# The two SwiGLU output projections of a trunk layer, computed as seven Strassen products instead of plain blocks

## The chip, the core and the metric

One core of one Trainium2 chip runs the whole program. The metric is the device time of one execution in microseconds (us). Five engines work at once and wait for each other through semaphores: TensorE (PE) multiplies matrices into PSUM, VectorE (DVE) and ScalarE (ACT) work elementwise, GpSimd (POOL) does elementwise work in SBUF only, and SyncE (SP) issues all DMA transfers of this kernel from one queue. Each engine takes its instructions in the order in which they were written for it.

## The reference, cut to what matters

A trunk layer has two SwiGLU blocks with a mixing block between them. There are 1280 tokens: 1024 latent ones and 256 of context. The change concerns `@ w_out` inside `swiglu`, where the inner dimension is D_FF = 2816 and the output has D_MODEL = 1024 features.

```python
def swiglu(x, w_in, w_out):
    a, b = jnp.split(x @ w_in, 2, axis=-1)
    return (jax.nn.silu(a) * b) @ w_out

def trunk_layer(x, cvec, lp, ctx):
    ...
    h = rmsnorm(x, lp['norm_g'][0]) * (1.0 + sc1) + sh1
    x = x + 0.5 * g1 * swiglu(h, lp['ffn_w_in'][0], lp['ffn_w_out'][0])
    h = rmsnorm(x, lp['norm_g'][1]) * (1.0 + sc2) + sh2
    ...
    x = x + g2 * y
    h = rmsnorm(x, lp['norm_g'][2]) * (1.0 + sc3) + sh3
    x = x + 0.5 * g3 * swiglu(h, lp['ffn_w_in'][1], lp['ffn_w_out'][1])
```

## The kernel before

**Layout.** Activations lie with features on the 128 partitions and tokens along the free dimension. The tokens come in three chunks: `CHUNKS` 0 and 1 are 512 latent tokens each, chunk 2 is the 256 context tokens. `x[c][d]` is the residual stream of chunk c, feature tile d of 8; it is in SBUF during a projection. A matrix product keeps float32 accuracy with three float32r matmuls: an operand is split into a rounded part (a cast on ACT: `whi`, `uh`) and the rest (a subtraction on DVE: `wlo`, `ul`), and high by high, high by low and low by high are added up in PSUM.

**Stages.** `up(0)` computes silu(a)·b of the first SwiGLU, 22 inner tiles j one after the other, by seven products each (`seven`, on 512 latent tokens and half of the 1024 input features) and two plain context products; it writes the results to `ud` in DRAM. `down(0)` is the second projection. Then come the norm (`norm_chunk`), the input projection of the mixing block (its first products are called `pa_`), the mixing stages, the output projection, `up(1)` and `down(1)`, whose result is stored as `out_yT`. The program below calls `down(0)` the first half and `down(1)` the second half.

**The projection, `down`.** It runs over 11 blocks of two inner tiles (`BL = 2`). In a block it loads two rows of `w2` of 1024 columns and the two matching rows of `ud`, splits them, and for each chunk and each of 8 feature tiles accumulates six matmuls in one PSUM tile `po`. DVE then multiplies this tile by the gate and adds it to `x` (a SCALAR_TENSOR_TENSOR `x<-po,modT,x`). So in each block every tile of `x` is updated once: 264 updates in a projection. After the last block of a chunk, `done` is called: in the first half the norm of this chunk, in the second half the stores.

**Tiles.** `HG` hands out 40 buffers of 128x512 (raw loads `ur` among them), `TG` 28, of which 20 hold `x` during a projection. `whi` and `wlo` have 4 buffers each of 1024 columns. PSUM has two pools of 4 banks, `PG` and `PT_`.

**Order of work.** The program is first written down as a list; then a list scheduler (`Plan.issue`) sets the order of each engine with costs and latencies of its own (`price`, `LAT`): it takes the earliest written instruction that is ready when an engine becomes free. So an edit in one place can move instructions in others. All instructions are issued from one line, 394, which is why rows of the profile are told apart by the names of their tiles.

**Modulation.** While `up(0)` runs, `mod_half` computes 7 of the 9 modulation vectors beside it, in 112 portions: POOL multiplies twice (`pr<-wh,cb`, `wh<-wh,cb`), ACT sums up each product, and DVE adds the two sums to `modT` (128x2).

## Time and profile before

| what | value |
|---|---|
| time, median of 3 runs | 2585.28 us (2583.64 to 2587.88) |
| profiled execution | 2589.14 us, span 2587.4 us |
| PE busy | 2491.5 us, 96% of the span |
| DVE busy | 1762.7 us, 68% |
| ACT busy | 1011.8 us, 39% |
| POOL busy | 572.3 us, 22% |
| read from and written to HBM | 195.11 MB and 61.87 MB, 99 GB/s over the span |

The span runs from the first to the last instruction; the time of an execution has 1.7 us more around it. A busy PE is not a PE at its peak, since matmuls overlap: the pitch from start to start says what one costs. The profiled execution is 3.9 us above the median of the three runs.

### The profile page before, as it was taken

The numbers are of one execution on the slowest core, as the hardware profiler recorded it, in microseconds if no ns is written. First come the engines' busy times: TensorE is split into PE (matmuls) and PEld (weight loads), VectorE is DVE, ScalarE is ACT, GpSimd is POOL, SyncE is SP. The second block draws the span as 40 slices with busy tenths as digits, with TensorE's granted clock in tenths as the row PEclk, the third lists the DMA queues.
The fourth block names the chain that finished last, engine by engine and source line by source line (L and its number), as shares of the span: only waits on it lengthen the run. The fifth ranks groups of instructions, "written<-read, shape, count | busy, mean of one in ns | idle before, by whom it ended". The sixth has DMA issues, their size and how long they took to land.

```text
span 2587.4 us, 37285 instructions
## 1 busy us (share of the span) xinstructions
PE 2491.5 (96%) x14100; PEld 2096.2 (81%) x14100; DVE 1762.7 (68%) x2819; ACT 1011.8 (39%) x2009; POOL 572.3 (22%) x475
## 2 busy tenths in 40 slices
PE   5899999999999999999999989979999999999999
PEld 3688888888888878888778778868888888888888
DVE  7988888876877674568656575385555555587765
ACT  6555555543212046242476685252222222232110
POOL 1578778830000031122100263130000000000000
PEclk8899999999999999999999999979999999999999
DMA  7143444435422132341301234212122221362312
GB/s 262 60 141 118 146 126 143 124 104 185 150 78 86 49 106 68 103 124 66 109 31 36 81 114 142 98 37 80 54 80 67 66 74 60 97 234 86 94 50 82
DMA packets 146676, 259.42 MB, mean 100 GB/s; under 512 B 15936, under 2 KB 61504, under 8 KB 146496
## 3 DMA queue, kind: packets, MB, share of 16 engines
q1 hardware_dynamic: 146496, 257.04, 31.0%
q8 instruction: 111, 1.82, 0.3%
q14 instruction: 69, 0.57, 0.1%
HBM read 195.11 MB, written 61.87 MB: 99 GB/s over the span
## 4 chain that ended last, share of the span: by engine, by line
PE 74%; DVE 4%; ACT 2%; DMA 1%; issue 1%; POOL 0%; SPq 0%; ACTq 0%
PE po L394 23%; PE p_t L394 12%; PE p_b L394 9%; PE px L394 6%; PE pwo L394 4%; PE fb L394 3%; PE pgd L394 3%; PE ptb L394 2%; PE pyb L394 2%; PE ps L394 2%; PE pd L394 1%; DVE x L394 1%; ACT prob L394 1%; DVE dst L394 1%; PE pgate L394 1%
## 5 line engine op out<-in xcount | busy, mean ns | idle before, releaser
L394 DVE SCALAR_TENSOR_TENSOR x<-po,modT,x 128x512 f32<-128x512 f32 (+1 forms) x528 | 345.3, 661 | 159.7 <-PE po L394 158.4
L394 PE MATMUL po<-uh,whi 128*128 128x512 f32 (+1 forms) x1056 | 377.5, 358 | 5.1 <-DVE x L394 5.1
L394 ACT CAST whi<-raw 128x1024 fp32r<-128x1024 f32 x206 | 213.7, 1048 | 424.7 <-PE px L394 142.2
L394 PE MATMUL po<-uh,wlo 128*128 128x512 f32 (+1 forms) x1056 | 375.3, 355 | 0.0
L394 PE MATMUL po<-ul,whi 128*128 128x512 f32 (+1 forms) x1056 | 373.2, 353 | 0.0
L394 DVE TENSOR_TENSOR wlo<-raw,whi 128x1024 fp32r<-128x1024 f32 x206 | 281.3, 1366 | 100.4 <-ACT whi L394 96.1
L394 PEld LDWEIGHTS po<-uh,whi 128*128 128x128 f32 x1056 | 199.7, 189 | 32.2 <-DVE x L394 5.8
L394 PEld LDWEIGHTS po<-uh,wlo 128*128 128x128 f32 x1056 | 199.3, 189 | 30.9
L394 PEld LDWEIGHTS po<-ul,whi 128*128 128x128 f32 x1056 | 199.5, 189 | 29.5
L394 PE MATMUL px<-hh,whi 128*128 128x256 f32 x704 | 200.2, 285 | 2.3 <-ACT uc L394 1.2
L394 PE MATMUL px<-hl,whi 128*128 128x256 f32 x704 | 200.0, 284 | 0.7 <-DVE hl L394 0.7
L394 PE MATMUL px<-hh,wlo 128*128 128x256 f32 x704 | 198.8, 282 | 0.0
L394 POOL TENSOR_TENSOR pr<-wh,cb 128x512 f32<-128x512 f32 x112 | 172.8, 1543 | 92.3 <-DMA wh<-in_wmodT 60.7
L394 POOL TENSOR_TENSOR wh<-wh,cb 128x512 f32<-128x512 f32 x112 | 186.6, 1666 | 8.8
L394 ACT CAST uh<-ur 128x512 fp32r<-128x512 f32 x110 | 67.3, 622 | 301.7 <-DMA ur<-ud 248.0
L394 POOL TENSOR_TENSOR sq<-sq,sq 128x512 f32<-128x512 f32 (+1 forms) x32 | 37.9, 1185 | 495.3 <-ACT sq L394 492.3
L394 PEld LDWEIGHTS px<-hh,whi 128*128 128x128 f32 x704 | 135.1, 192 | 6.8 <-ACT hh L394 1.6
L394 PEld LDWEIGHTS px<-hl,whi 128*128 128x128 f32 x704 | 134.8, 192 | 5.4 <-DVE hl L394 1.3
L394 PEld LDWEIGHTS px<-hh,wlo 128*128 128x128 f32 x704 | 134.5, 191 | 0.5
L394 ACT ACTIVATE g<-g 128x512 f32<-128x512 f32 x88 | 55.6, 632 | 177.7 <-DVE g L394 177.6
L394 ACT ACTIVATE pr<-pr 128x512 f32<-128x512 f32 x112 | 70.9, 633 | 83.4 <-POOL pr L394 71.4
L394 ACT ACTIVATE wh<-wh 128x512 f32<-128x512 f32 x112 | 70.5, 629 | 56.6 <-POOL wh L394 55.8
(511 smaller groups left out, 6113.3 us busy)
## 6 DMA issues: line engine op xcount, KB each, us to landing
raw<-in_w SPq DMA_DIRECT2D x132, 512.0 KB
wh<-in_wmodT SPq DMA_DIRECT2D x112, 256.0 KB
ur<-ud SPq DMA_DIRECT2D x88, 256.0 KB
ud<-v SPq DMA_DIRECT2D x44, 256.0 KB
ud<-u SPq DMA_DIRECT2D x44, 256.0 KB
x<-in_xT SPq DMA_DIRECT2D x32, 256.0 KB
wmt<-in_wmod SPq DMA_DIRECT2D x32, 256.0 KB
xs<-x SPq DMA_DIRECT2D x32, 256.0 KB
```

The source lines that it names most:

```text
L394: getattr(real, meth)(*[f(v) for v in a], **{q: f(v) for q, v in k.items()})
```

## The change

Both projections are computed as one 2x2 block product: the inner dimension is cut into two halves of 11 tiles (`HF`), the output features into two halves of four tiles, and the latent tokens are chunks 0 and 1. Seven passes make the seven Strassen products, each over 11 inner tiles, with four PSUM tiles that collect the whole inner sum; one more pass (the fourth) has no latent product. The operands of five passes are sums or differences of weight tiles or activation tiles (`s1` to `s4`, `t1` to `t4`); DVE makes them as 128x512 tiles, and some are kept (`keep`) for a later pass. A finished PSUM tile is added to the outputs that need this product, 1 to 4 of them. The context is not part of it: half of its features are computed beside the first two passes with the same split weights (`pc`), the other half in the fourth pass. Splits of weights are now 512 columns wide. `done` is called for a chunk and a half of its features; in the first half all three norms are written behind the last pass, and the `pa_` products take the context chunk first. The addition to `modT` goes from DVE to POOL. Two small tables are written down in another place.

```diff
@@ -595,7 +595,7 @@
         S.activation(pr, pr, AF.Identity, accum_out=part[:, 0:1])
         G.tensor_tensor(w, w, cbs[0][:, 1], ALU.mult)
         S.activation(w, w, AF.Identity, accum_out=part[:, 1:2])
-        V.tensor_tensor(modT[:, s, f], part, modT[:, s, f] if hf else smv("bmod", 8 * s + f).to_broadcast([P, 2]),
+        G.tensor_tensor(modT[:, s, f], part, modT[:, s, f] if hf else smv("bmod", 8 * s + f).to_broadcast([P, 2]),
                         ALU.add)
         if hf and f == KT - 1:
             mod_finish(s)
@@ -705,7 +705,8 @@
-    BL = 2
+    HF = NFF // 2
     RAW = 2
     rawp = None
     ud = dp.tile([NFF, P, T], F32, name="ud")
@@ -821,40 +822,133 @@
             if after_unit:
                 after_unit()
-    def down(n, gate, src, after_block=None, done=None):
-        nb = NFF // BL
-        for b in range(nb):
-            js = [b * BL + jj for jj in range(BL)]
-            us = [[None] * 3 for _ in js]
...
-            for c, (t0, w) in enumerate(CHUNKS):
-                v = 1 if c == 2 else 0
-                for d in range(KT):
-                    po = PG("po")
-                    ds_ = slice(d * P, (d + 1) * P)
-                    for i in range(BL):
-                        (uh, ul), (hi, lo) = us[i][c], wo[i]
-                        TE.matmul(po[:, :w], hi[:, ds_], uh, start=(i == 0), stop=False)
-                        TE.matmul(po[:, :w], hi[:, ds_], ul, start=False, stop=False)
-                        TE.matmul(po[:, :w], lo[:, ds_], uh, start=False, stop=(i == BL - 1))
-                    V.scalar_tensor_tensor(x[c][d], po[:, :w], modT[:, gate, d, v:v + 1], x[c][d], ALU.mult, ALU.add)
-                if b == nb - 1:
-                    done(c)
+    def down(n, gate, src, done):
+        w2 = I["w2"][n]
+        c11, c12, c21, c22 = (0, 0), (1, 0), (0, 1), (1, 1)
+        lo, hi = slice(0, 512), slice(512, 1024)
+        keep = {}
+        def get(src_):
+            r = HG(name="ur")
+            dma(r, src_)
+            return r
+        def b(k, half, cols):
+            return get(ud[HF * half + k][:, cols])
+        def a(k, half, cols):
+            return get(w2[HF * half + k][:, cols])
+        def less(p, q, out):
+            V.tensor_tensor(out, p, q, ALU.subtract)
+            return out
+        def s1(k):
+            p, q = a(k, 0, hi), a(k, 1, hi)
+            V.tensor_tensor(p, p, q, ALU.add)
+            keep["s", k] = p
+            return p
+        def t1(k):
+            p = b(k, 0, hi)
+            keep["t", k] = less(p, b(k, 0, lo), p)
+            return p
+        def s2(k):
+            return less(keep["s", k], a(k, 0, lo), keep["s", k])
+        def t2(k):
+            return less(b(k, 1, hi), keep["t", k], keep["t", k])
+        def t4(k):
+            p = b(k, 1, lo)
+            return less(p, keep["t", k], p)
+        def s3(k):
+            p = a(k, 0, hi)
+            return less(p, a(k, 0, lo), p)
+        def t3(k):
+            p, q = b(k, 0, hi), b(k, 1, hi)
+            keep["b", k] = q
+            return less(p, q, p)
+        def s4(k):
+            p = a(k, 1, lo)
+            return less(p, keep["s", k], p)
+        PASSES = [
+            (lambda k: a(k, 1, lo), lambda k: b(k, 1, lo), [c11], (1, 0)),
+            (lambda k: a(k, 0, lo), lambda k: b(k, 0, lo), [c11, c12, c21, c22], (0, 0)),
+            (s1, t1, [c12, c22], None),
+            (lambda k: a(k % HF, k // HF, hi), None, [], (0, 1)),
+            (s2, t2, [c12, c21, c22], None),
+            (lambda k: a(k, 1, hi), t4, [c21], None),
+            (s3, t3, [c21, c22], None),
+            (s4, lambda k: keep["b", k], [c12], None),
+        ]
+        left = {}
+        for _, _, outs, _ in PASSES:
+            for o in outs:
+                left[o] = left.get(o, 0) + 1
+        def products(ps, wh, wl, q0, uh, ul, first, last):
+            for d in range(4):
+                q = slice(q0 + d * P, q0 + (d + 1) * P)
+                TE.matmul(ps[d], wh[:, q], uh, start=first, stop=False)
+                TE.matmul(ps[d], wh[:, q], ul, start=False, stop=False)
+                TE.matmul(ps[d], wl[:, q], uh, start=False, stop=last)
+        def update(c, f, p):
+            v = 1 if c == 2 else 0
+            V.scalar_tensor_tensor(x[c][f], p, modT[:, gate, f, v:v + 1], x[c][f], ALU.mult, ALU.add)
+        pc = None
+        for i, (ws, us, outs, context) in enumerate(PASSES):
+            nk = NFF if us is None else HF
+            ps = [(PG if i in (0, 1, 3, 5, 7) else PT_)(name="po") for _ in range(4)] if us is not None else None
+            if i in (0, 3):
+                pc = [(PT_ if i == 0 else PG)(name="pc")[:, :256] for _ in range(4)]
+            for k in range(nk):
+                q0 = 512 * (k % 2)
+                if context:
+                    if k % 2 == 0:
+                        j = k + HF * context[0] if us is not None else k
+                        m = min(2, nk - k)
+                        r, ch, cl = HG(name="ur"), HG(F32R, "uch"), HG(F32R, "ucl")
+                        dma(r[:, :256 * m].rearrange("p (j n) -> p j n", j=m),
+                            ud[j:j + m, :, NLAT:T].rearrange("j p n -> p j n"))
+                        split(ch[:, :256 * m], cl[:, :256 * m], r[:, :256 * m])
+                if k % 2 == 0:
+                    wh = wp.tile([P, 1024], F32R, name="whi", tag="whi", bufs=4)
+                    wl = wp.tile([P, 1024], F32R, name="wlo", tag="wlo", bufs=4)
+                split(wh[:, q0:q0 + 512], wl[:, q0:q0 + 512], ws(k))
+                if us is not None:
+                    r = us(k)
+                    uh, ul = TG(F32R, "uh"), TG(F32R, "ul")
+                    split(uh, ul, r)
+                if i == 0 and k == 0:
+                    for c in range(3):
+                        load_x(c, src)
+                if context:
+                    q = slice(256 * (k % 2), 256 * (k % 2) + 256)
+                    products(pc, wh, wl, q0, ch[:, q], cl[:, q], k == 0 and i != 1, k == nk - 1 and i != 0)
+                if us is not None:
+                    products(ps, wh, wl, q0, uh, ul, k == 0, k == nk - 1)
+            if i in (1, 3):
+                for d in range(4):
+                    update(2, 4 * context[1] + d, pc[d])
+                done(2, context[1])
+            for d in range(4):
+                for c, h in outs:
+                    update(c, 4 * h + d, ps[d])
+            for o in outs:
+                left[o] -= 1
+                if left[o] == 0:
+                    done(*o)
     held = []
     ops1 = Ops()
@@ -925,10 +1019,6 @@
         S.activation(g128, lgp, AF.Exp, scale=128.0)
         V.tensor_scalar(zeta, zeta, 0.125, None, ALU.mult)
-    def after(b):
-        if b == 2:
-            tables()
-
     nu = [0]
     def after_unit():
@@ -943,17 +1033,20 @@
     xs = dp.tile([KT, P, T], F32, name="xs")
     h2 = {}
-    def done1(c):
+    def done1(c, half):
         t0, w = CHUNKS[c]
+        for d in range(4 * half, 4 * half + 4):
+            dma(xs[d][:, t0:t0 + w], x[c][d])
         if not h2:
             h2[0] = ([None] * 3, [None] * 3)
-        norm_chunk(1, *h2[0], c)
-        for d in range(KT):
-            dma(xs[d][:, t0:t0 + w], x[c][d])
+            tables()
+        if (c, half) == (1, 0):
+            for c in (2, 0, 1):
+                norm_chunk(1, *h2[0], c)
     up(0, ops1, prepare, after_unit)
     assert not mods
-    down(0, 2, None, after_block=after, done=done1)
+    down(0, 2, None, done1)
     hh, hl = h2[0]
@@ -992,7 +1085,8 @@
         V.memset(xa[f][:, 1026:1029], 0.0)
         V.memset(xa[f][:, 1285:1286], 0.0)
         ga[f] = T5(name=f"ga{f}")
-    for c, (t0, n) in enumerate(CHUNKS):
+    for c in (2, 0, 1):
+        t0, n = CHUNKS[c]
         for i in (0, 2, 1, 3):
             ps = PG("pa_")
             gemm_fm(ps, *wA[i], hh, hl, c)
@@ -1709,13 +1803,13 @@
             for kk in range(4):
                 (ops2.second_half if c else ops2.first_half)(2, kk)
-    def done2(c):
+    def done2(c, half):
         t0, w = CHUNKS[c]
-        for d in range(KT):
+        for d in range(4 * half, 4 * half + 4):
             dma(O["yT"][:, d, t0:t0 + w], x[c][d])
     up(1, ops2)
-    down(1, 8, xs, done=done2)
+    down(1, 8, xs, done2)
     closed(rawp)
     closed(tg)
     closed(wp)```

How the order of instructions moves is shown at three places. The first is DVE in the second half. Before, around the end of a block (`ul` and `wlo` are the low parts of activations and weights, `x_...` the residual tiles):

```order
L394 TENSOR_TENSOR ul<-ur,uh 128x512
L394 SCALAR_TENSOR_TENSOR x_20846<-po,modT,x_20846 128x512
L394 SCALAR_TENSOR_TENSOR x_20851<-po,modT,x_20851 128x256 x2
L394 SCALAR_TENSOR_TENSOR x_20854<-po,modT,x_20854 128x256 x2
L394 TENSOR_TENSOR ul<-ur,uh 128x512
L394 SCALAR_TENSOR_TENSOR x_20859<-po,modT,x_20859 128x256 x2
L394 SCALAR_TENSOR_TENSOR x_20862<-po,modT,x_20862 128x256
L394 TENSOR_TENSOR ul<-ur,uh 128x512
L394 SCALAR_TENSOR_TENSOR x_20862<-po,modT,x_20862 128x256
L394 TENSOR_TENSOR wlo<-raw,whi 128x1024
```

After the change, at the end of the second pass (`pc` and `po` are finished products):

```order
L394 TENSOR_TENSOR wlo<-ur,whi 128x512 x2
L394 TENSOR_TENSOR ucl<-ur,uch 128x512
L394 TENSOR_TENSOR ul<-ur,uh 128x512
L394 TENSOR_TENSOR ucl<-ur,uch 128x512
L394 TENSOR_TENSOR ul<-ur,uh 128x512
L394 SCALAR_TENSOR_TENSOR x_21086<-pc,modT,x_21086 128x256 x2
L394 SCALAR_TENSOR_TENSOR x_21089<-pc,modT,x_21089 128x256 x2
L394 SCALAR_TENSOR_TENSOR x_20952<-po,modT,x_20952 128x512
L394 SCALAR_TENSOR_TENSOR x_21055<-po,modT,x_21055 128x512
L394 SCALAR_TENSOR_TENSOR x_20972<-po,modT,x_20972 128x512
L394 SCALAR_TENSOR_TENSOR x_21069<-po,modT,x_21069 128x512
L394 SCALAR_TENSOR_TENSOR x_20955<-po,modT,x_20955 128x512
```

Updates of `x` stood in every block, one for each finished product; now 20 of them (four of 256 columns, sixteen of 512) stand in one piece between the second and the third pass. By then the rows ahead of them hold 25 low parts `ul` of activations and 26 `wlo`, 22 of each for the first two passes: three inner tiles of the third pass are split ahead of the updates. The 22 sums of the third pass (`ur<-ur`) stand ahead of them too.

The second place is PE at the end of the first half (`nst` and `nrs` are the two small products of a norm). Before:

```order
L394 MATMUL po<-uh,wlo 128x256
L394 MATMUL po<-uh,whi 128x256
L394 MATMUL nst<-ones,sq_8423 128x1 x4
L394 MATMUL po<-ul,whi 128x256
L394 MATMUL po<-uh,wlo 128x256
L394 MATMUL po<-uh,whi 128x256
L394 MATMUL po<-ul,whi 128x256
L394 MATMUL po<-uh,wlo 128x256
L394 MATMUL pa__8699<-hh_7945,whi 128x512
```

After:

```order
L394 MATMUL po<-uh,whi 128x512
L394 MATMUL po<-ul,whi 128x512
L394 MATMUL po<-uh,wlo 128x512
L394 MATMUL nst<-ones,sq_8473 128x1 x2
L394 MATMUL nst<-ones,sq_8565 128x1 x4
L394 MATMUL nrs<-dg,ones 128x128 x6
L394 MATMUL pa__8873<-hh_8481,whi 128x256
L394 MATMUL pa__8882<-hh_8481,whi 128x256
L394 MATMUL pa__8890<-hh_8481,whi 128x256
```

Before, projection products of the context stand between the norms of earlier chunks, and the first `pa_` product is of 512 latent tokens. Now nothing stands on PE between the last projection product and the context norm that the first `pa_` product needs.

The third place is POOL in the opening of the program, where the last operands of `up(0)` are made (`t3l`, `t4l`, four pairs) beside the first portions of the modulation. Before:

```order
L394 TENSOR_TENSOR pr<-wh,cb 128x512
L394 TENSOR_TENSOR wh<-wh,cb 128x512
L394 TENSOR_TENSOR t3l<-x_108,t3h 128x512
L394 TENSOR_TENSOR t4l<-x_85,t4h 128x512
L394 TENSOR_TENSOR t3l<-x_109,t3h 128x512
L394 TENSOR_TENSOR t4l<-x_86,t4h 128x512
L394 TENSOR_TENSOR t3l<-x_110,t3h 128x512
L394 TENSOR_TENSOR t4l<-x_87,t4h 128x512
L394 TENSOR_TENSOR pr<-wh,cb 128x512
```

After:

```order
L394 TENSOR_TENSOR pr<-wh,cb 128x512
L394 TENSOR_TENSOR wh<-wh,cb 128x512
L394 TENSOR_TENSOR pr<-wh,cb 128x512
L394 TENSOR_TENSOR t3l<-x_109,t3h 128x512
L394 TENSOR_TENSOR t4l<-x_86,t4h 128x512
L394 TENSOR_TENSOR modT<-part,small 128x2
L394 TENSOR_TENSOR wh<-wh,cb 128x512
L394 TENSOR_TENSOR pr<-wh,cb 128x512
L394 TENSOR_TENSOR modT<-part,small 128x2
L394 TENSOR_TENSOR wh<-wh,cb 128x512
L394 TENSOR_TENSOR t3l<-x_110,t3h 128x512
L394 TENSOR_TENSOR t4l<-x_87,t4h 128x512
```

Between the first and the last of these pairs two products of the modulation stood on POOL; now there are eight, and five additions to `modT`, each of which waits for ACT.

## Rows read from the trace of the kernel before

**Rows 1.** The page: busy time of each engine; the chain that ended last, by engine.

```profile
PE 2491.5 (96%) x14100; PEld 2096.2 (81%) x14100; DVE 1762.7 (68%) x2819; ACT 1011.8 (39%) x2009; POOL 572.3 (22%) x475
...
PE 74%; DVE 4%; ACT 2%; DMA 1%; issue 1%; POOL 0%; SPq 0%; ACTq 0%
PE po L394 23%; PE p_t L394 12%; PE p_b L394 9%; PE px L394 6%; PE pwo L394 4%; PE fb L394 3%; PE pgd L394 3%; PE ptb L394 2%; PE pyb L394 2%; PE ps L394 2%; PE pd L394 1%; DVE x L394 1%; ACT prob L394 1%; DVE dst L394 1%; PE pgate L394 1%
```

**Rows 2.** Chain in order of time: start us, length us, what, instructions.

```profile
644.10 292.21 PE po L394 x1509
...
1001.53 5.49 PE pa__9016 L394 x24
...
1015.50 2.83 PE pa__9151 L394 x24
...
2279.99 304.05 PE po L394 x1584
```

**Rows 3.** Windows: engines' busy us (instructions), granted clock, DMA share, GB/s.

```profile
130.00:644.00 514.00, 504.56 (x2639) 429.56 (x2638) 412.08 (x476) 268.17 (x588) 332.81 (x208) 0.99 0.43 135
...
2280.00:2588.00 308.00, 304.02 (x1584) 260.31 (x1583) 220.73 (x331) 45.98 (x63) 0.00 (x0) 1.00 0.29 94
```

**Rows 4.** DVE's groups by form in 2280 to 2588 us.

```profile
L394 DVE SCALAR_TENSOR_TENSOR x<-po,modT,x 128x512 f32<-128x512 f32 x176 | 131.3, 750 | 70.5 <-PE po L394 69.9
L394 DVE SCALAR_TENSOR_TENSOR x<-po,modT,x 128x256 f32<-128x256 f32 x88 | 42.0, 483 | 12.0 <-PE po L394 12.0
L394 DVE TENSOR_TENSOR ul<-ur,uh 128x512 fp32r<-128x512 f32 x47 | 32.0, 686 | 1.0 <-PE po L394 1.0
```

**Rows 5.** DVE's timeline: start us, length us, what, instructions in a row.

```profile
941.43 2.06 DVE L394 SCALAR_TENSOR_TENSOR nt<-x,scl,nrs 128x512 f32<-128x512 f32 x3
943.41 0.77 DVE L394 SCALAR_TENSOR_TENSOR hl<-nt,modT,hh 128x512 fp32r<-128x512 f32 x1
...
2280.36 1.29 DVE L394 TENSOR_TENSOR ul<-ur,uh 128x512 fp32r<-128x512 f32 x2
2281.57 0.75 DVE L394 SCALAR_TENSOR_TENSOR x<-po,modT,x 128x512 f32<-128x512 f32 x1
```

**Rows 6.** Windows where the DMA engines are busiest.

```profile
2280.00:2290.00 10.00, 10.00 (x45) 8.18 (x45) 9.23 (x14) 2.00 (x3) 0.00 (x0) 1.00 0.98 332
2290.00:2300.00 10.00, 10.00 (x46) 8.19 (x45) 8.55 (x14) 4.36 (x7) 0.00 (x0) 1.00 0.83 291
```

**Rows 7.** Timeline, PE at the end of the first half.

```profile
948.70 0.39 PE L394 MATMUL po<-uh,whi 128*128 128x256 f32 x1 [3.19 <-DVE x L394]
...
954.05 0.41 PE L394 MATMUL po<-uh,whi 128*128 128x256 f32 x1
954.27 0.41 PE L394 MATMUL po<-ul,whi 128*128 128x256 f32 x1
```

**Rows 8.** Timeline, DVE in the norms behind it.

```profile
960.93 1.22 DVE L394 TENSOR_TENSOR wlo<-raw,whi 128x1024 fp32r<-128x1024 f32 x1
...
973.51 0.15 DVE L394 RECIPROCAL rt<-rt 128x2 f32<-128x2 f32 x1
973.70 1.31 DVE L394 TENSOR_SCALAR dg<-ident,rt 128x128 f32<-128x128 f32 x2
975.76 1.26 DVE L394 SCALAR_TENSOR_TENSOR nt<-x,scl,nrs 128x256 f32<-128x256 f32 x3 [0.74 <-PE nrs L394]
```

**Rows 9.** POOL's groups by form in 920 to 985 us.

```profile
L394 POOL TENSOR_TENSOR sq<-sq,sq 128x512 f32<-128x512 f32 x10 | 12.9, 1294 | 390.2 <-ACT sq L394 388.4 <-DVE nt L394 1.6
...
L394 POOL TENSOR_TENSOR sq<-sq,sq 128x256 f32<-128x256 f32 x4 | 3.1, 764 | 1.0 <-ACT sq L394 0.9
```

**Rows 10.** Timelines of DVE and POOL in the opening.

```profile
73.27 0.69 DVE L394 TENSOR_TENSOR b22l<-x,b22h 128x512 fp32r<-128x512 f32 x1
...
76.42 1.80 DVE L394 TENSOR_TENSOR x<-x,x 128x512 f32<-128x512 f32 x1
...
76.38 1.29 POOL L394 TENSOR_TENSOR t3l<-x,t3h 128x512 fp32r<-128x512 f32 x1 [6.26 <-ACT t3h L394]
```

**Rows 11.** DVE's groups by form, 145 to 640 us; PE's waits, 104 to 644 us.

```profile
L394 DVE TENSOR_TENSOR modT<-part,modT 128x2 f32<-128x2 f32 x56 | 44.2, 789 | 14.0 <-ACT wh L394 14.0
L394 DVE TENSOR_TENSOR modT<-part,small 128x2 f32<-128x2 f32 x46 | 38.5, 836 | 12.9 <-ACT wh L394 12.9
...
PE p_t L394 <- DVE u L394: 9.4, 5, 3.4
```

**Rows 12.** DVE's last update, at the end of the program (timeline).

```profile
2584.06 0.48 DVE L394 SCALAR_TENSOR_TENSOR x<-po,modT,x 128x256 f32<-128x256 f32 x1 [0.22 <-PE po L394]
```

More of the change, by code (lines that the diff above doesn't have):

```diff
@@ L822, in up @@
                 after_unit()
-    def down(n, gate, src, after_block=None, done=None):
-        nb = NFF // BL
-        for b in range(nb):
-            js = [b * BL + jj for jj in range(BL)]
-            us = [[None] * 3 for _ in js]
-            wo = [load_split(I["w2"][n, j]) for j in js]
-            for c, (t0, w) in enumerate(CHUNKS):
-                views = [] if c == 2 else [[i] for i in range(BL)]
-                if c == 2:
-                    views = [list(range(BL))]
-                for js_ in views:
-                    r, hi, lo = HG(name="ur"), HG(F32R, "uh"), HG(F32R, "ul")
-                    for q, i in enumerate(js_):
-                        dma(r[:, q * w:(q + 1) * w], ud[js[i]][:, t0:t0 + w])
-                        us[i][c] = (hi[:, q * w:(q + 1) * w], lo[:, q * w:(q + 1) * w])
-                    split(hi, lo, r)
-            if b == 0:
-                for c in range(3):
-                    load_x(c, src)
-            if after_block:
-                after_block(b)
-            for c, (t0, w) in enumerate(CHUNKS):
-                v = 1 if c == 2 else 0
-                for d in range(KT):
-                    po = PG("po")
-                    ds_ = slice(d * P, (d + 1) * P)
-                    for i in range(BL):
-                        (uh, ul), (hi, lo) = us[i][c], wo[i]
-                        TE.matmul(po[:, :w], hi[:, ds_], uh, start=(i == 0), stop=False)
-                        TE.matmul(po[:, :w], hi[:, ds_], ul, start=False, stop=False)
-                        TE.matmul(po[:, :w], lo[:, ds_], uh, start=False, stop=(i == BL - 1))
-                    V.scalar_tensor_tensor(x[c][d], po[:, :w], modT[:, gate, d, v:v + 1], x[c][d], ALU.mult, ALU.add)
-                if b == nb - 1:
-                    done(c)
```

## Prediction

> **What bounds the kernel now.** I read the page first: PE is busy for 96% of the span and makes 74% of the chain that ended last, the projections alone (`po`) 23% [rows 1]. An engine so full need not be the limit in each stage, so I went on to the chain in order of time. There the whole second half is one link of PE, 1584 matmuls in 304.05 us without a wait [rows 2], while DVE is busy 220.73 us, ACT 45.98 us and DMA moves 94 GB/s [rows 3]. So in the projections the number of matmuls sets the time, and a matmul costs its pitch. The `pa_` links give it: 24 of 512 columns in 5.49 us, 0.2288 each; 24 of 256 columns in 2.83 us, 0.118 each [rows 2]. As a test: the second half has 1056 and 528 of them, 1056×0.2288 + 528×0.118 = 303.9 us, and 304.05 was measured. At the granted clock of 1.00 [rows 3] nothing faster is to be had of a single matmul.
>
> **What the change removes.** Per half there remain 7 products × 11 inner tiles × 4 feature tiles × 3 = 924 matmuls of 512 columns instead of 1056; the 528 of the context stay. 132×0.2288 = 30.2 us in each half: **−60.4 us in all**. A half should then take 273.7 us on PE: two passes with context of 45.8, one of context alone of 31.2 and five of 30.2.
>
> **What it adds on DVE.** Updates fall from 264 to 64 a half (56 of 512 columns, 8 of 256). Two-input operations on 512 columns become 99 `wlo`, 77 `ul`, 23 `ucl` and 88 sums, 287 together. In a row such an operation costs 0.605 us and an update 0.66, from start to start [rows 5]; the durations are 0.686 and 0.750 [rows 4]. So DVE has 214 us by pitch and 243 by durations, for PE's 273.7. On average it keeps pace; the question is where it is bunched.
>
> *The burst behind the second pass.* 20 updates stand in one piece, sixteen of 512 and four of 256 columns. The four can start when the context products are done and fit before the first product of 512 columns is; that is 9 matmuls, 2.06 us, before the end of the pass. Then 16×0.66 = 10.6 us (16×0.75 = 12.0), less 2.06, leaves 8.5 to 9.9 us, and one `ul` more (0.6 to 0.69) makes 9.1 to 10.6. Meanwhile PE has the three inner tiles split ahead, 3×12×0.2288 = 8.2 us. A stall of 0.9 to 2.4 us a half; I take 2: **+4**.
>
> *The passes with sums.* In the third, fifth and seventh pass an inner tile asks four operations of DVE, 2.42 us by pitch and 2.74 by durations, and 2.75 of PE. Over the last four passes DVE has 111 to 126 us for PE's 121, after a lead of three to four inner tiles (8 to 11 us). I take nothing; the cover is that lead, and without it the difference of up to 5 us a half shows.
>
> **The end of the first half.** Before, from 644.10 to the end of the `pa_` products at 1018.33 (1015.50 + 2.83) there are 374.2 us [rows 2]. PE's own work in it is 304.05 + 8×5.49 + 4×2.83 = 359.3, so 14.9 us are lost: PE waited 3.19 us for an update, and ran 256-column matmuls at 0.21 to 0.22 us, nearly twice their pitch, after such waits [rows 7]. Now PE has nothing between its last product and the context norm. DVE needs about 0.2 + 0.75 for the last update, 1.22 for a `wlo`, 0.3 for two reciprocals, six `dg` (0.65 each in a pair [rows 8]; as little as a third of that if they overlap, so 1.3 to 3.9), 0.74 for PE's `nrs` and 0.48 for the first `nt`; with some 0.6 for ACT's `hh` that is 5.6 to 8.2 us. The first `pa_` product is then paced by DVE, which needs 16 operations of 256 columns at 0.39 (three in 1.26 us [rows 8]), 6.2 us, where PE needs 2.83: another 3.4. Together 9 to 11.6, I take 10.9 against 14.9: **−4**, bounds −6 and +1.
>
> **The lock of POOL in that last pass.** The three norms add 10 squares of 512 columns at 1.294 us and 5 of 256 at 0.764 on POOL [rows 9], 16.7 us, now beside a pass whose DVE work is all two-input operations. Alone a two-input operation on 512 columns took 0.69 us, beside a POOL operation 1.80 [rows 10]: it waited for nearly all of POOL's 1.29. At worst all 16.7 us are added to the 25 us of DVE in that pass, 42 for PE's 30.2 and its lead of 8 to 11; DVE also waits for POOL's sums in its own order, with `ul` queued behind. 0 to 12 us; I take **+3**, since the lead swallows most. The Trainium skill ("SBUF — State Buffer", "Who interferes with whom") calls this an exclusive lock: a DVE operation with two inputs in SBUF and a GpSimd one that reads SBUF never overlap, and the loser fully blocks. By that rule the worst case above would be the normal one; this trace agrees on the single pair (1.80 for 0.69).
>
> **`modT` on POOL.** DVE loses 102 shown additions in `up(0)` at 789 and 836 ns, 82.7 us [rows 11], of 412.08 busy; POOL has 332.81 of 514 us [rows 3] and takes them. PE waited for DVE's `u` 9.4 us in five places there [rows 11]. At best all of it goes, at worst nothing, and DVE is then no less late behind POOL's lock: **−5**.
>
> **The opening.** Six more modulation products (and five additions that wait for ACT) stand between the `t3l`/`t4l` pairs. At about 1.3 to 1.6 us (POOL's 1.29 for an operation of this size [rows 10], and a wait for DVE's two-input operations) up to 9.6 us, if PE has no other product ready. I take **+3**, nearer to the low end, since seven products of other operands stand ahead of the last ones.
>
> **The end.** The last update is of 512 columns, 0.75 [rows 4] for 0.48 [rows 12], and its store is twice as large: **+0.6**.
>
> **Sum.** −60.4 + 4 − 4 + 3 − 5 + 3 + 0.6 = −58.8. The profiled execution took 2587.4 + 1.7 = 2589.1 us, so 2530.3; it was 3.9 above the median of the runs, so **2526** as a median. All bounds at their best give −60.4 + 1.8 − 6 − 9.4 + 0.5 = −73.5 (2512); all at their worst −60.4 + 4.8 + 10 + 1 + 12 + 9.6 + 1 = −22 (2563).
>
> **The rivals.**
> *DVE becomes the bound where it is bunched (17%).* DVE runs at its durations and POOL's lock bites in full. For it: the fifth and seventh pass leave it no margin (2.74 for 2.75). Against it: DVE's pitch in a row is well under its durations [rows 5]. The stalls are then 5 a burst, 5 a half in the passes with sums, 12 at the lock: −60.4 + 10 + 10 + 12 − 4 + 3 + 0.6 = −29: **2556**; with half of it 2541.
> *All is covered (10%).* The leads are longer than I count and the norm's gap is short: the best bounds above and 2 to 8 us of other waits that go with the DVE load in `up(0)`, where PE is busy 504.56 of 514 us [rows 3]: **2504 to 2512**.
> *DMA is late, and the kernel slower (5%).* Weights and activations are no longer loaded once but for each pass: 209 loads of 262,144 bytes and 44 portions of 131,072 are 60.6 MB a half, with `x` in and out (10.5) 71.0; before 94 GB/s were moved [rows 3], now 71.0/273.7 = 260 GB/s are needed, in the third and seventh pass 44×0.262/30.2 = 382. The busiest stretch shows 332 GB/s at a share of 0.98 [rows 6], so these passes must be loaded ahead, in 40 buffers of which up to 22 hold kept operands. Against it: over three passes each (the first to third, the fifth to seventh) the need is about 255. It decides below 71.0/304 = 233 GB/s: if half-rows of weights and one queue that waits for free buffers bring the mean to 220, a half takes 323 us, 19 more than now: **2623**.
> *A removed matmul is worth less than its pitch (3%).* If waits of PE that the trace hides in the pitch stay, the gain is perhaps half: **2555**. The test sum above speaks against it.
> *No change (3%).* DMA near 235 GB/s, by the same sum.
>
> **The numbers.** The forecast has 62%, the rest as above. A measurement of this kernel tells about 0.2%, 5 us, from no change; only the last-named case falls within that, and only late DMA is slower: faster 92%, same 3%, slower 5%. The forecast's own bounds are 2512 to 2545; to leave out no more than 2 in 10 the range takes in a part of the covered case and most of DVE's: **2509 to 2555**.
>
> **What would show it.** Right: 924 + 528 products a half in about 274 us of PE; a wait of PE for DVE's `ul` of 1 to 2.4 us behind the second pass; a gap of 6 to 8 us ahead of the first `pa_`; no wait for `u` in `up(0)`; DMA's share high in the third and seventh pass without a wait of ACT or DVE for `ur`. Wrong: PE waiting for `wlo` or `ul` all through a pass with sums (DVE is the bound, or, if `whi` waits for `ur`, DMA is); a two-input DVE operation of 1.8 us repeated in the last pass with PE idle behind it; a granted clock that falls in these gaps, which would make the matmuls behind them cost twice.

## The result and the profile after

The changed kernel takes 2558.5 us (median of 4 runs, 2557.3 to 2564.5) where the kernel before takes 2584.5 beside it: the ratio is 0.9903, with a 95% interval of 0.9884 to 0.9922. It is faster, by 26 us, less than half of the 58.8 that were forecast, and lies 3.5 us above the range. The profiled execution took 2557.47 us, 31.7 less than that of before, which lies 4.7 us above the median beside it.

The page of the changed kernel, busy time, as in [rows 1]:

```profile
PE 2444.4 (96%) x13836; PEld 2048.7 (80%) x13836; DVE 1693.5 (66%) x2727; ACT 1130.1 (44%) x2256; POOL 606.3 (24%) x587
```

PE is as full as before, with 264 matmuls less. On the page its share of the chain that ended last fell from 74 to 70%, and DVE's and DMA's rose by a point each. The second half, in the chain in order of time and in the windows (columns as in [rows 2, 3]):

```profile
2376.59 21.73 PE po L394 x92
2398.32 29.92 PE pc L394 x264
2428.24 121.11 PE po L394 x519
```

```profile
2274.00:2552.00 278.00, 277.06 (x1455) 234.44 (x1454) 209.45 (x341) 106.35 (x185) 0.00 (x0) 1.00 0.66 228
```

The last four passes are one link of PE, and PE is busy for 277.06 us where it was for 304.02 [rows 3]. DMA moves 228 GB/s instead of 94 without appearing among PE's waits.

**Where the time went.** Five starting times from PE's timeline of each profiled execution: the first projection product of the first half, its last one, the first `pa_` product, the last `pa_` matmul, and the first product of the second half; then the span.

| kernel | 1st half | its end | first `pa_` | last `pa_` | 2nd half | span |
|---|---|---|---|---|---|---|
| before | 643.94 | 959.62 | 959.74 | 1018.05 | 2279.82 | 2587.4 |
| after | 648.42 | 927.42 | 937.43 | 1009.75 | 2274.17 | 2555.4 |
| second_half_only | 637.22 | 951.65 | 951.77 | 1010.50 | 2277.50 | 2560.7 |
| modT_pool_before | 646.78 | 961.69 | 961.81 | 1020.11 | 2284.64 | 2592.2 |
| modT_on_dve | 642.39 | 921.60 | 931.59 | 1003.65 | 2267.71 | 2550.1 |
| pa_other_banks | 648.19 | 928.31 | 938.31 | 997.33 | 2263.14 | 2545.5 |
| order_012 | 647.63 | 927.74 | 940.01 | 1003.22 | 2268.49 | 2549.9 |
| ctx_norm_early | 647.44 | 940.90 | 941.94 | 1015.08 | 2282.22 | 2563.4 |
| stats_early | 645.90 | 934.49 | 935.34 | 1007.86 | 2277.53 | 2559.9 |
| banks_modT | 641.13 | 919.83 | 929.82 | 988.85 | 2256.83 | 2538.2 |
| stats_early_021_modT | 640.45 | 926.38 | 926.66 | 987.99 | 2249.50 | 2532.4 |
| stats_mid_021_modT | 641.03 | 924.88 | 925.94 | 989.02 | 2253.22 | 2534.4 |

Before and after: up(0) ends 4.5 us later; the first half's products take 279.2 us; but the `pa_` products end only 8.3 us earlier than before, where 30.2 were to be saved. The second half then keeps its own saving: it starts 5.7 us earlier, and the span is 32.0 shorter.

**The stretch behind the first half.** PE's timeline:

```profile
927.42 0.39 PE L394 MATMUL po<-uh,wlo 128*128 128x512 f32 x1
927.65 1.39 PE L394 MATMUL nst<-ones,sq 128*128 128x1 f32 x12
933.50 1.22 PE L394 MATMUL nrs<-dg,ones 128*128 128x128 f32 x4 [4.45 <-DVE dg L394]
...
937.43 0.58 PE L394 MATMUL pa__8873<-hh,whi 128*128 128x256 f32 x1
...
941.01 0.41 PE L394 MATMUL pa__8873<-hl,whi 128*128 128x256 f32 x1
941.23 0.41 PE L394 MATMUL pa__8873<-hh,wlo 128*128 128x256 f32 x1
...
942.48 0.28 PE L394 MATMUL pa__8873<-hl,whi 128*128 128x256 f32 x1
942.59 0.28 PE L394 MATMUL pa__8873<-hh,wlo 128*128 128x256 f32 x1
942.71 0.95 PE L394 MATMUL nst<-ones,sq 128*128 128x1 f32 x8
943.52 0.36 PE L394 MATMUL pa__8873<-hh,whi 128*128 128x256 f32 x1
...
951.83 0.28 PE L394 MATMUL pa__8897<-hh,wlo 128*128 128x256 f32 x1
...
963.30 0.80 PE L394 MATMUL pa__9211<-hh,whi 128*128 128x512 f32 x1 [9.36 <-ACT xa L394]
...
964.32 0.63 PE L394 MATMUL pa__9211<-hh,wlo 128*128 128x512 f32 x1
964.75 0.63 PE L394 MATMUL pa__9211<-hh,whi 128*128 128x512 f32 x1
```

Four losses can be read off. First 9.8 us (927.65 to 937.43) until the context's first `pa_`. Then the context's four products take 14.5 us for 11.3 of work, 3.2 lost: behind the gap some twenty of their matmuls start 0.21 us apart, later ones 0.12, which makes 2.0, and the small products of the latent norms (`nst`, `nrs`) stand between them with 1.2. Then PE has hardly any work from 951.95 to 963.30, 11.35 us, of which 9.36 are one wait, for ACT's copy `xa`. And behind it the first matmuls start 0.43 us apart, from 969 us on 0.23: PE was granted its lower level (1.2 GHz) after standing still, and the eight products of the latent chunks take 46.7 us instead of 43.9. Together 27.1 us, where 14.9 were lost before and 10.9 were forecast. ACT's timeline shows why `xa` was late:

```profile
961.45 0.62 ACT L394 CAST hh<-nt 128x512 fp32r<-128x512 f32 x1
962.18 0.72 ACT L394 ACTIVATE hh<-nt,modT 128x512 fp32r<-128x512 f32 x1
962.88 0.38 ACT L394 COPY xa<-pa__8873 128x256 f32<-128x256 f32 x1
```

The context's first `pa_` tile, `pa__8873`, was finished near 946 us, but its copy out of PSUM stands in ACT's order behind the activations of both latent chunks' norms, and each of these waits for a DVE `nt`. All four banks of the pool hold finished context products, so PE cannot begin chunk 0. The kernel before had its copies behind the norms as well (ACT's timeline):

```profile
981.35 0.57 ACT L394 COPY xa<-pa__8699 128x512 f32<-128x512 f32 x1
```

This is the copy of its first `pa_` tile. But there the first four products are of 512 columns, and the last of them ran until 985.05 us, so no bank was missing.

**The opening.** Windows of the changed kernel, then POOL's timeline there:

```profile
100.00:110.00 10.00, 7.69 (x34) 6.06 (x34) 9.96 (x11) 5.61 (x12) 8.10 (x6) 0.84 0.17 52
110.00:120.00 10.00, 10.00 (x40) 8.05 (x40) 7.60 (x9) 5.15 (x13) 7.92 (x8) 0.89 0.34 111
```

```profile
104.05 0.63 POOL L394 TENSOR_TENSOR modT<-part,small 128x2 f32<-128x2 f32 x1 [1.90 <-ACT wh L394]
...
108.00 2.27 POOL L394 TENSOR_TENSOR t4l<-x,t4h 128x512 fp32r<-128x512 f32 x1
```

POOL waits 1.90 us for ACT with an addition to `modT`, and the last operand `t4l` is ready only at 110.27 us. Between the first `t3l`/`t4l` pair and the last, four additions to `modT` stand in the trace, not five.

### The profile page after: what moved, and what is told of

The parts are those of the page before. It is cut to its first block, busy times and chain, and to the rows that moved or that the text cites. A ratio compares the mean times of both kernels' runs of the same rounds, so it can differ in the third digit from the quotient of the medians.

```text
span 2555.4 us, 37638 instructions
## 1 busy us (share of the span) xinstructions
PE 2444.4 (96%) x13836; PEld 2048.7 (80%) x13836; DVE 1693.5 (66%) x2727; ACT 1130.1 (44%) x2256; POOL 606.3 (24%) x587
## 4 chain that ended last, share of the span: by engine, by line
PE 70%; DVE 5%; DMA 2%; ACT 2%; issue 1%; POOL 0%; SPq 0%; ACTq 0%; DVEq 0%
PE po L394 16%; PE p_t L394 12%; PE p_b L394 9%; PE px L394 6%; PE pc L394 4%; PE pwo L394 4%; PE fb L394 3%; PE pgd L394 3%; PE ptb L394 3%; PE pyb L394 2%; PE ps L394 2%; DVE x L394 1%; PE pd L394 1%; PE dpa L394 1%; ACT prob L394 1%
## 5 line engine op out<-in xcount | busy, mean ns | idle before, releaser
L394 DVE TENSOR_TENSOR wlo<-raw,whi 128x1024 fp32r<-128x1024 f32 x162 | 224.3, 1385 | 142.6 <-ACT whi L394 135.0
L394 ACT CAST whi<-raw 128x1024 fp32r<-128x1024 f32 x162 | 169.2, 1045 | 298.6 <-PE px L394 140.7
L394 PE MATMUL po<-ul,whi 128*128 128x512 f32 x616 | 243.9, 396 | 2.1 <-DVE ul L394 2.1
L394 PE MATMUL po<-uh,wlo 128*128 128x512 f32 x616 | 243.5, 395 | 0.0
L394 PE MATMUL po<-uh,whi 128*128 128x512 f32 x616 | 240.3, 395 | 0.0
L394 PE MATMUL px<-hh,whi 128*128 128x256 f32 x704 | 200.0, 284 | 2.3 <-ACT uc L394 1.2
L394 PE MATMUL px<-hl,whi 128*128 128x256 f32 x704 | 200.0, 284 | 0.7 <-DVE hl L394 0.7
L394 PE MATMUL px<-hh,wlo 128*128 128x256 f32 x704 | 199.0, 283 | 0.5 <-DVE wlo L394 0.5
L394 POOL TENSOR_TENSOR pr<-wh,cb 128x512 f32<-128x512 f32 x112 | 175.2, 1564 | 36.1 <-DMA wh<-in_wmodT 13.0
L394 ACT CAST whi<-ur 128x512 fp32r<-128x512 f32 x198 | 117.9, 619 | 135.7 <-DVE ur L394 47.5
L394 POOL TENSOR_TENSOR wh<-wh,cb 128x512 f32<-128x512 f32 x112 | 171.2, 1529 | 4.1
L394 ACT CAST uh<-ur 128x512 fp32r<-128x512 f32 x154 | 94.5, 620 | 173.8 <-PE po L394 110.8
L394 DVE TENSOR_TENSOR ul<-ur,uh 128x512 fp32r<-128x512 f32 x154 | 106.2, 691 | 79.4 <-ACT uh L394 65.8
L394 DVE TENSOR_TENSOR wlo<-ur,whi 128x512 fp32r<-128x512 f32 x198 | 133.7, 693 | 27.5 <-ACT whi L394 27.0
L394 PEld LDWEIGHTS px<-hh,whi 128*128 128x128 f32 x704 | 135.2, 192 | 7.0 <-ACT hh L394 1.6
L394 PEld LDWEIGHTS po<-ul,whi 128*128 128x128 f32 x616 | 115.7, 188 | 29.8 <-DVE ul L394 3.6
L394 PEld LDWEIGHTS px<-hl,whi 128*128 128x128 f32 x704 | 134.9, 192 | 5.5 <-DVE hl L394 1.3
L394 PEld LDWEIGHTS po<-uh,wlo 128*128 128x128 f32 x616 | 115.7, 188 | 27.4
L394 PEld LDWEIGHTS po<-uh,whi 128*128 128x128 f32 x616 | 115.4, 188 | 26.3 <-ACT uh L394 0.2
L394 PEld LDWEIGHTS px<-hh,wlo 128*128 128x128 f32 x704 | 134.8, 192 | 1.5 <-DVE wlo L394 0.9
L394 ACT ACTIVATE g<-g 128x512 f32<-128x512 f32 x88 | 55.3, 629 | 153.7 <-DVE g L394 153.7
L394 DVE TENSOR_TENSOR ur<-ur 128x512 f32<-128x512 f32 x176 | 117.1, 703 | 0.3 <-DMA ur<-in_w 0.2
```

Of the source, the lines that this page charges most:

```text
L394: getattr(real, meth)(*[f(v) for v in a], **{q: f(v) for q, v in k.items()})
```

## The experiments

**The second half alone.** The new projection as a function of its own, called for `down(1)` only.

```diff
-    down(1, 8, xs, done=done2)
+    down_s(1, 8, xs, done2)
```

> Edit: the kernel before, with the new projection in the second half alone. Theory (the products are worth what was forecast, the first half's gain is lost around them): the second half of the changed kernel takes 277 us where 304 were; the kernel gains 27 less 0.6 at the end: 2556 to 2559, as much as the whole change. Rival (the two halves gain alike, some 13 us each): 2570 to 2573.

Measured: 2560.8 us, ratio 0.9908 (0.9881 to 0.9935). The windows of its second half:

```profile
2277.00:2557.00 280.00, 278.78 (x1458) 235.44 (x1456) 209.19 (x341) 106.33 (x185) 0.00 (x0) 1.00 0.66 226
```

That is 2 us above the first expectation and far from the other. Within the intervals half of the change gains as much as the whole, so the first half, the boundary behind it and `modT` together come to about nothing.

**`modT` alone, on the kernel before.**

```diff
-        V.tensor_tensor(modT[:, s, f], part, ...
+        G.tensor_tensor(modT[:, s, f], part, ...
```

> Edit: the kernel before, with the addition to modT on POOL and nothing else. Theory (POOL's order in the opening costs, DVE's relief beside up(0) gives nothing): slower by 4 to 8 us: 2588 to 2592. Rival (the cost came from the shift of other work by the new projection): no change, 2582 to 2586.

Measured: 2593.8 us, ratio 1.0036 (1.0023 to 1.0050), slower by 9.4 us, a little more than expected. And the same line undone in the changed kernel:

> Edit: the addition to modT goes back to DVE, nothing else. Theory (POOL's order in the opening): up(0) ends 4.5 us later in the changed kernel because POOL makes more modulation portions between the last operands t3l and t4l; with the addition on DVE that order is that of before, and the kernel gains 3 to 6 us: 2552 to 2556. Rival (the addition is worth something beside up(0)): DVE loses 80 us again and its u is later, no gain or a loss of up to 4: 2558 to 2562.

Measured: 2551.1 us, ratio 0.9865 (0.9849 to 0.9882), 7.5 below the changed kernel. Its windows and POOL's timeline at the same place:

```profile
100.00:110.00 10.00, 9.21 (x38) 7.02 (x39) 9.56 (x13) 4.25 (x6) 4.14 (x2) 1.00 0.08 29
110.00:120.00 10.00, 10.00 (x56) 8.62 (x55) 6.46 (x9) 4.53 (x11) 4.89 (x4) 1.00 0.68 197
```

```profile
102.42 2.27 POOL L394 TENSOR_TENSOR t4l<-x,t4h 128x512 fp32r<-128x512 f32 x1
```

`t4l` is ready at 104.69 instead of 110.27, PE idles less and its clock is back at 1.00 from 100 us on, not 0.84 and 0.89. Over all twelve profiled executions the first half starts at 641.0 us on the mean with the addition on DVE (six kernels, 637.2 to 643.9) and at 647.4 with it on POOL (six, 645.9 to 648.4). A single pair tells less: before and `modT_pool_before` are only 2.8 us apart there. Both directions agree: the line costs 6 to 9 us.

**Other banks for chunk 0.**

```diff
-            ps = PG("pa_")
+            ps = (PT_ if c == 0 else PG)(name="pa_")
```

> Edit: the four pa_ products of chunk 0 take their PSUM tiles from the other pool of four banks, so that they need not wait until the context's four are copied out. Theory (PSUM held): in the changed kernel PE waits 9.36 us ahead of the first pa_ of chunk 0 because the copies of the context products stand on ACT behind the norm's activations, and then runs at half the clock; without that wait chunk 0 starts near 952 us, paced by DVE, and the kernel gains 8 to 11 us: 2548 to 2551. Rival (norm paced by DVE): chunk 0's nt and hl are finished only near 960 us anyway, PE waits for them instead; gain 0 to 3 us: 2555 to 2559.

Measured: 2547.0 us, ratio 0.9850 (0.9835 to 0.9864), 11.6 below the changed kernel. The chain in order of time:

```profile
959.26 5.49 PE pa__9035 L394 x24
...
992.22 5.28 PE pa__9286 L394 x23
```

The wait for `xa` is gone, and the latent products run on end at 5.49 us each, at the full clock: the last `pa_` starts at 997.33 instead of 1009.75, and the stretch loses 13.8 us instead of 27.1. The rival, that DVE's norm would hold PE just as long, is out.

**The order of before.** Norms and `pa_` products run over chunks 0, 1, 2.

```diff
-            for c in (2, 0, 1):
+            for c in range(3):
                 norm_chunk(1, *h2[0], c)
...
-    for c in (2, 0, 1):
-        t0, n = CHUNKS[c]
+    for c in range(3):
+        t0, n = CHUNKS[c]
```

> Edit: norms and pa_ products at the end of the first half in the order of before, chunks 0, 1, context. Theory (the boundary ate the first half's gain, by its order): chunk 0 is complete one pass earlier, its norm can be made beside the last pass, PE has 22 us of pa_ work at once while the others are normed; of the 27 us lost between the last projection product and the end of the pa_ products 10 to 20 come back: 2539 to 2549. Rival (DVE is full): the norm's work for chunk 0 only moves into the last pass, whose products then wait for ul and wlo; gain under 4 us: 2555 to 2560.

Measured: 2551.8 us, ratio 0.9871 (0.9857 to 0.9886), 6.7 gained, between the two expectations. The wait for the banks is gone, but the gap ahead of the first `pa_` grew to 12.0 us (927.74 + 0.23 to 940.01), by PE's waits there:

```profile
PE nrs L394 <- DVE dg L394: 7.8, 5, 5.6
```

My reason for the edit was wrong: chunk 0 was complete early, yet its norm stands behind all products of the last pass in PE's order, since these were written first.

**The context's norm earlier.**

```diff
-        if (c, half) == (1, 0):
-            for c in (2, 0, 1):
+        if (c, half) == (2, 1):
+            norm_chunk(1, *h2[0], 2)
+        if (c, half) == (1, 0):
+            for c in (0, 1):
                 norm_chunk(1, *h2[0], c)
```

> Edit: the context's norm is written behind the fourth pass, where the context is complete, order of the rest as in the changed kernel. Theory (gap ahead of the first pa_): the 9.8 us between the last projection product and the first pa_ product go, since the context's operands are ready; but the wait for chunk 0 behind it grows by a part of that; gain 3 to 9 us: 2549 to 2556. Rival (chunk 0's norm sets the time): no gain, the wait only moves: 2557 to 2560. A second rival: 8 buffers less for loads in the last four passes, DMA late, slower by 2 to 6.

Measured: 2564.8 us, ratio 0.9921 (0.9906 to 0.9935). By the medians it is 6.2 slower than the changed kernel, though the two intervals overlap; it gains nothing, in any case. PE's waits from 645 to 1025 us:

```profile
PE pa__9211 L394 <- ACT xa L394: 9.3, 1, 9.3
PE po L394 <- DVE ul L394: 5.8, 4, 2.9
PE po L394 <- DVE nt L394: 3.0, 1, 3.0
```

The gap of 9.8 us fell to 0.8, and the wait for `xa` stayed. But the fifth pass waited for DVE's norm and the sixth for `ul`, and the half's products end 13.5 us later. Loads were not the reason: from 806 to 870 us DVE is idle for 2.8 us in all and never for a load, and in the chain twelve updates (7.99 us from 843.52) stand ahead of the `ul` that PE waited 2.85 us for. That the norm's work had used up DVE's lead is the likely reason; it was not tried alone.

**The statistics earlier.** Only the sums of squares and the root of chunks 2 and 0, ahead of the last pass.

```diff
+        if (c, half) == (0, 1):
+            for c in [2, 0]:
+                norm_stats(c)
         if (c, half) == (1, 0):
             for c in (2, 0, 1):
-                norm_chunk(1, *h2[0], c)
+                norm_chunk(1, *h2[0], c, stat=c == 1)
```

> Edit: the sums of squares, the two small products and the reciprocal root of the context and of chunk 0 are written ahead of the last pass, where both are complete; the normed operands stay behind it. Theory (two separate waits): the 9.8 us ahead of the first pa_ product fall to 1 to 3, the last pass pays 0 to 2 for the POOL sums, and the wait of 9.4 us ahead of chunk 0 stays, for its cause (copies behind the norm's activations) is untouched; gain 4 to 8 us: 2550 to 2555. Rival (one chain sets both, the normed operands of chunk 0): the second wait grows by what the first loses; gain under 2: 2557 to 2560.

Measured: 2561.3 us (2553.1 to 2562.4), ratio 0.9908 (0.9883 to 0.9933): no gain. PE's and DVE's timelines at the start of the last pass:

```profile
899.07 1.01 PE L394 MATMUL nst<-ones,sq 128*128 128x1 f32 x4 [4.63 <-DVE x L394]
...
900.94 0.63 PE L394 MATMUL po<-uh,whi 128*128 128x512 f32 x1
901.37 0.63 PE L394 MATMUL po<-ul,whi 128*128 128x512 f32 x1
...
897.62 5.34 DVE L394 SCALAR_TENSOR_TENSOR x<-po,modT,x 128x512 f32<-128x512 f32 x8
```

The gap ahead of the first `pa_` did fall, to 0.6 us (934.49 + 0.23 to 935.34). But `nst` needs one of four banks that eight updates of the pass before still hold, and the projection products behind it stand still with it, then go on at 0.43 us apart. The first half's products took 9.6 us longer. Of these the stop and the lower clock behind it make 6.6, again for a PSUM tile, and the norm's own small products some 2. The wait for `xa` stayed at 9.2 us, as the first expectation has it; only the gain was lost in the last pass.

**The parts together.** First the two single repairs (`modT` on DVE, other banks):

> Edit: the two single repairs together, chunk 0's pa_ products in the other four banks and the addition to modT on DVE. Theory (the two losses are separate): 11.6 and 7.5 us add up against the changed kernel: 2538 to 2542. Rival (they share a part, for up(0) only shifts what the boundary waits for): 2545 to 2550.

Measured: 2538.9 us, ratio 0.9812 (0.9787 to 0.9838). Expected from the sum of the two: 2539.4. The losses are separate. Then early statistics, `pa_` products in the order 0, 2, 1 with the context's in the other banks, and `modT` on DVE:

> Edit: the statistics as in the run beside it, the addition to modT on DVE, pa_ products in the order chunk 0, context, chunk 1, the context's in the other four banks. If the parts add up: 7.5 us of the opening, some 8 ahead of the first pa_ and some 10 of the wait for the banks come back, and PE has 22 us of work of chunk 0 while chunk 1 is normed: 2528 to 2536. If the waits share one cause (DVE's norm work): 2537 to 2546.

Measured: 2534.7 us, ratio 0.9815 (0.9791 to 0.9839), within what the parts add up to. Last the same with the statistics written behind the sixth inner tile of the last pass:

```diff
+                if mid and i == 7 and k == 5:
+                    mid()
...
-    down(0, 2, None, done1)
+    down(0, 2, None, done1, lambda: [norm_stats(c) for c in (0, 2)])
```

> Edit: the best kernel so far with the statistics of chunk 0 and the context written behind the sixth inner tile of the last pass instead of ahead of the pass, by when the updates that hold the four banks for nst are done. Theory (nst waited for a bank that the updates of the pass before still held, 4.6 us in one run and 3.0 in the other, then half the clock): these waits go, 2528 to 2533. Rival (the norm's work on DVE and ACT is what slows that pass): ul or wlo is late instead, 2533 to 2538.

Measured: 2533.5 us (2528.9 to 2536.2), ratio 0.9798 (0.9781 to 0.9815), the best kernel of the study, 25 us below the changed one; that it beats the one before it, or the two single repairs, the intervals don't show. It lies between its two expectations: the wait of `nst` for a bank is gone, but PE still loses 2.3 us to `dg` and 1.8 to `sq`, now beside the last pass.

## Why the prediction was wrong

**The saving was right.** Per half the forecast was 273.7 us of products and 2 of stalls. The second half took 277.1 (2274.17 to 2551.04 + 0.23), the first 279.2, with POOL's lock forecast at 3. Several sizes in it were off and nearly cancel. The matmuls of the new projection start 0.2333 us apart (519 in 121.11 us), not 0.2288: 924 of them cost 4.2 us more. The 256-column ones of the fourth pass start 0.113 apart (264 in 29.92), not 0.118, so more was to be had of a matmul than its pitch in `pa_`; over all 528 that gives back 1.3. And the burst of 20 updates came as forecast, sixteen in 10.62 us, but cost PE 0.37 us in each half, not 2; the sum left out that four products of the fourth inner tile need no `ul`. In the second half:

```profile
2363.75 1.65 DVE L394 SCALAR_TENSOR_TENSOR x<-pc,modT,x 128x256 f32<-128x256 f32 x4
2365.32 10.62 DVE L394 SCALAR_TENSOR_TENSOR x<-po,modT,x 128x512 f32<-128x512 f32 x16
2375.85 0.68 DVE L394 TENSOR_TENSOR ul<-ur,uh 128x512 fp32r<-128x512 f32 x1
...
2376.59 0.50 PE L394 MATMUL po<-ul,whi 128*128 128x512 f32 x1 [0.37 <-DVE ul L394]
```

The passes with sums cost nothing, as forecast: PE's waits for `ul` come to 2.1 us over both halves, and the two bursts have 0.7 of them and the very first pass 1.1.

**The step that failed: "The end of the first half", −4 with bounds −6 and +1.** It measured +12.2 (27.1 lost for 14.9). The sum ended with the first `pa_` product: 5.6 to 8.2 us of gap (9.8 measured) and 3.4 for a first product paced by DVE. That 3.2 were lost there is luck: PE waited for no operand in the context's products, and what they lost is the lower clock and the norms' small products. The sum then took the other eleven products at their pitch and never asked where the four finished context tiles go. Their copies stand on ACT behind the norms' activations, which are written ahead of them, as they were before; but the context's four products, at 2.8 us each, now come first and fill all four banks before the norm of chunk 0 is through. That is 11.35 us, and the lower clock behind it 2.8 more. Shown: other banks alone give 11.6 us back. The gap itself was 1.6 us over its upper bound. The chain through it:

```profile
930.26 1.28 ACT L394
...
932.18 4.27 DVE dg L394 x6
```

The six `dg` took 4.27 us, above the bound of 3.9. And from PE's last product to 931.82 the chain stands on ACT, 4.2 us with a `whi`, two squares, a table load of 1.28 (the first line) and the root; the sum had 2.2 us of DVE there and of ACT only the `hh`.

The Trainium skill ("Perfetto Trace Analysis", "Optimizing Tensor Performance") says that independent groups of matmuls should rotate through different banks so that the copy of one overlaps the next. The changed kernel does rotate, through four; this trace shows that it helps only as far as the copying engine is free in its own order, 9.36 us of waiting with four banks and none with eight.

**The second: the opening, +3, and `modT` on POOL, −5.** Together −2 was forecast, 4.5 later was measured, and over all kernels 6.4. The opening was mis-sized: I let the low end rule because PE had other products ready. The last `t4l` came 5.6 us later and PE had to wait for nearly all of it, in idle time and lower clock. The relief was no relief: in up(0) PE waits 9.7 us for `u`, ten times, where it waited 9.4 [rows 11], though DVE was busy 70 to 76% instead of 83 to 86%. Over the six kernels of each kind these waits come to 7.6 to 9.7 us with the addition on POOL and 5.5 to 10.2 with it on DVE, so they do not follow DVE's load; what they are for stays open.

**What remains.** Between the `pa_` products and the second half 2.7 us more were lost. That part of the program is the same in all kernels, and over the twelve executions it took 1261.5 to 1269.7 us, 1261.8 in the one of before, so it tells nothing. The terms then add up: 6.5 us missed in up(0), 16.2 behind the first half, 2.7 here, about 2 in the projections, 27.4 by these roundings of the 27.1 that were missed between the profiled executions. By the medians 32.9 were missed; the other 5.8 are how far the two profiled executions lie from their medians.

**The rivals.** DVE as the bound gave 2556, close to the time by another way: its waits are not in the profile. POOL's lock was real and cost next to nothing. Beside the squares DVE's sums took longer, and the squares too (1.60 us and 1.1 on the mean for 256 columns, 0.764 in [rows 9]):

```profile
L394 DVE TENSOR_TENSOR ur<-ur 128x512 f32<-128x512 f32 x25 | 19.4, 814 | 0.0
...
881.58 1.60 POOL L394 TENSOR_TENSOR sq<-sq 128x256 f32<-128x256 f32 x1 [341.25 <-ACT sq L394]
883.26 4.51 POOL L394 TENSOR_TENSOR sq<-sq,sq 128x256 f32<-128x256 f32 x4
```

814 ns are some 130 more than in the second half (685), where POOL is idle. The Trainium skill's lock ("SBUF — State Buffer", "Who interferes with whom") agrees, but not that DVE bears all of it: by these means DVE's two-input operations lost some 5 us from 865 to 928 us, and the ten squares that ran there about as much. The lead of the splits covers it: the last four passes took 123.7 us in the first half and 123.2 in the second. DMA was hardly late. No wait of PE names it in either half, but the 1.1 us for `ul` in the first pass of the first half lead in the chain to loads. Its share was high in the first two passes and the fourth to sixth (1.02 and 0.91 at most), not in the third and seventh, which the prediction had named (0.27 and 0.47): so the loads ran ahead.

## What to carry to other kernels

When a change reorders who comes first at a boundary, follow each finished PSUM tile to the copy that frees it, and count what stands ahead of that copy on its engine; a sum that ends with the first product misses it. Short products fill the banks sooner than long ones: with the small chunk first four banks were too few here, with a long chunk first they were enough. A tiny operation moved to an idle engine is paid for by what is queued behind it there: look at that engine's order where its results are on the path, not at its mean load.

## What the runs showed of the hardware

After a stop of 9.36 us, and of 4.63 in the run with early statistics, PE's matmuls of 512 columns started 0.43 us apart instead of 0.23; after stops of 0.37 and 1.12 us they did not. The windows of the changed kernel give the granted clock, first behind the gap ahead of the context's products, then behind the stop of 9.36 us:

```profile
938.00:942.00 4.00, 4.00 (x22) 4.00 (x21) 2.76 (x8) 2.32 (x7) 1.70 (x2) 0.55 0.00 0
963.30:968.30 5.00, 5.00 (x12) 3.98 (x13) 0.73 (x8) 4.95 (x9) 1.40 (x2) 0.50 0.85 281
970.00:976.00 6.00, 6.00 (x28) 4.93 (x27) 3.44 (x13) 3.97 (x13) 0.00 (x0) 1.00 0.01 2
```

0.50 is the lower of the two levels (1.2 GHz). By the starts it lasted 5.3 us behind the stop, to 968.6, and 4.2 behind the gap, to 941.6, so a wait can cost more than its own length. Its length alone does not decide: behind 3.00 us in the run with the early context norm the matmuls were slow as well, and behind 3.19 in the kernel before [rows 7] they ran on at 0.12 us and slowed only behind a further wait of 1.66.

A matmul of 512 columns cost 0.2288 us in `pa_` (24 into one PSUM tile) and 0.2333 in the new projection (three into one tile, then three into the next). Products of up(0) show both as well, 24 in 5.51 and in 5.60 us. One of 256 columns cost 0.118 in `pa_` and 0.113 in the fourth pass. What sets these differences was not tried.
